# Second-vector modulation, pair seeding and gates moved between VectorE and ScalarE in a two-layer conv, attention and SwiGLU kernel

## The chip, the cores and the metric

The kernel runs on one core of a Trainium2 chip. The metric is the device time of one execution in microseconds (us), as the median of several runs. Engines are named as in the profile: PE (TensorE, matmuls), PEld (its weight loads), DVE (VectorE), ACT (ScalarE), POOL (GpSimd) and SP (SyncE, whose queue issues the large loads).

## The reference, cut to what matters

Two layers work on 256 latent tokens and 256 context tokens of width 1024. Each layer is a half-weighted SwiGLU, a mixer (a short convolution in layer 0, grouped attention in layer 1) and another half-weighted SwiGLU. Every block is modulated by nine vectors per layer that come from a condition vector: one for the latents (`c`) and one for the context (`c_ctx`).

```
mod  = (silu(c)     @ mod_w[i] + mod_b[i]).reshape(bsz, 3, 3, 1, D_MODEL)
modc = (silu(c_ctx) @ mod_w[i] + mod_b[i]).reshape(3, 3, D_MODEL)
h    = rms(t, g) * (1 + scale) + shift
y    = (silu(h @ w1) * (h @ w3)) @ w2          # hidden width 2816 = 22 blocks of 128
t    = t + 0.5 * gate * y                      # for the mixers: t + gate * y
```

In layer 1 the context is needed only as keys and values, so its last modulation vectors and its last SwiGLU are not computed. All of it is float32.

## The kernel before

The activations stay transposed on the chip: `x` is 128 partitions x 8 blocks of the width x 512 tokens, of which columns 0 to 255 are latents (s = 0) and 256 to 511 context (s = 1). A float32 product is made of three matmuls (`mm3`): every operand is split into a rounded high part on ACT and the rest on DVE (`split`), and high x high, high x low and low x high are summed in PSUM.

Weights are loaded by SP in pieces of 128 x 2048 (1 MB) into a raw buffer (`load_raw`, tag `wr`, three buffers) and split into halves of 1024 columns (`half`, four buffers).

An FFN goes through its 22 hidden blocks in thirds of 8, 7 and 7. After each third, `project` multiplies that third with the second weight matrix, eight output blocks m = 0 to 7 of 128 x 512 (tile `py`), and `finish` adds gate x result to `x`, one DVE operation for each vector's 256 columns. In the last third the blocks 6 and 7 are done in token halves (`late`), so that the next norm can begin; `square_add` and `rms_inv` make that norm's sums.

In three of the four FFNs most hidden blocks are a `Pair`: the gate and the up block of one hidden index are the two rows of a 2 x 2 block product over (gate, up) x (two halves of the width) and (latents, context), which is computed with seven block products and sums of blocks in place of eight. `sums` of `Pair` makes the weight sums (in a tile `ws` of their own), `sums` of `Blocks` those of the activations. A product is 12 matmuls of 256 columns. One pair uses two PSUM banks: p and q. `head` puts the first product (A11) into p, which ACT copies to SBUF, and the second (A12) into the first half of q; `five` puts S1 into the second half of q, which ACT copies to `gm`; `six` adds S2 onto p (copied by ACT) and S4 onto the second half of q, then DVE adds q and the copies over 512 columns and ACT takes the SiLU; `seven` adds S3 onto p, which DVE turns into the second half of the up block; `four` adds A22, and DVE multiplies. A pair's `seven` and `four` stand between the products of the next pair. The first hidden blocks of an FFN are plain products (`w13_mm`, `w13_post`).

The modulation vectors are made beside this on DVE. Transposed modulation weights come in 64 pieces of two 1024-wide parts (`modT`); a unit (`mod_unit`) multiplies a part with one broadcast vector and sums it in one operation (junk tile, accumulator `mod`), so a piece has four units, or two where only the latents need it: 224 in all. `tick(n)` grants n units at places in the program; `mod_ready` forces what is missing when a vector is asked for (`gate_of`, `scale_of`). Ticks stand after each `finish` (1.5 to 1.7 each), in the convolution (6 for each of 8 blocks), in the q/k/v part (1, 1, 2), with each of the eight heads (2) and in the attention's output projection (1 each).

The start is different: the first modulation vectors come from PE (`mod_pe`, `mod_turn`, loads `mod0`), mixed with the first three hidden blocks in an order written out by hand (`FIRST_STEPS`). Elsewhere a planner lays out each engine's instructions from the program's order and its own costs; it may put an instruction that is ready before one that is not. Each engine then runs its list in that order. PSUM has eight banks: six results (`psum`, tag `mm`) and two small ones (`psmall`).

Of the kernel before, what the change touches and what calls it, by code (L numbers as in the profile page):

```python
# [16 lines left out]
P = 128  # L17
# [24 lines left out]
def hybrid_kernel(ctx: ExitStack, tc: tile.TileContext, a: dict, out: bass.AP):  # L42
# [7 lines left out]
    psm = ctx.enter_context(tc.tile_pool(name="psm", bufs=6, space=bass.MemoryType.PSUM))  # L50
# [9 lines left out]
    def psum(s="ps"):  # L60
        return psm.tile([P, T2], F32, tag="mm", name=nm(s))
# [30 lines left out]
    def load_raw(src, n=2048):  # L92
        raw = wp.tile([P, 2048], F32, name=nm("wr"), tag="wr", bufs=3)
        nc.sync.dma_start(raw[:, :n], src)
        return raw
# [11 lines left out]
    def load_w(src, n=2048, fine=False):  # L107
        raw = load_raw(src, n)
        hs = [half() for _ in range(0, n, 1024)]
        cuts = (0, 1024, 512, 1536) if fine else range(0, n, 1024)  # L110
# [52 lines left out]

    jobs = [(0, ch, p) for ch in range(2, 9) for p in range(4)]
# [4 lines left out]
    def next_unit():  # L169
        if not units:  # L170
            l, ch, pair = jobs.pop(0)
            mod_tile(l, ch)
            raw = load_raw(a["modT"][l, ch * 4 + pair])
            units.extend(
                (l, ch, pair, raw, j, v) for j in range(2) for v in range(streams(l, ch))
            )
        mod_unit(*units.pop(0))

    def tick(n):

        owed[0] += n
        while (jobs or units) and owed[0] >= 1:
            owed[0] -= 1
            next_unit()
# [31 lines left out]
    def square_add(k, c0, c1):  # L216
# [4 lines left out]
        for s in range(2):  # L221
            if c0 <= s * S < c1:
                part = sq[:, s * S - c0 : s * S - c0 + S]
                if k == 0:
                    accs[s] = tp.tile([P, S], F32, name=nm("acc"), tag=f"acc{s}", bufs=1)
                    nc.vector.tensor_copy(accs[s], part)
                elif k < KT - 1:
                    nc.vector.tensor_tensor(out=accs[s], in0=accs[s], in1=part, op=ALU.add)
                else:
                    accs[s, "last"] = part  # L230
# [165 lines left out]
    def tail_norm(l, j, h):  # L396
# [3 lines left out]
        def tail(m, c0, c1):  # L400
            square_add(m, c0, c1)
            if m == KT - 1:
# [5 lines left out]
                def inv():  # L408
                    return rms_inv(s, (accs[s], accs[s, "last"]))
# [31 lines left out]
    def finish(m, ps, c0, c1, gate, tail):  # L441
        g = gate()
        for s in range(2):
            if c0 <= s * S < c1:
                o = s * S - c0
# [72 lines left out]

    def w13_mm(pp, w, h, ks, c0, c1):
        for k in ks:  # L520
            mv = pick(h, k, c0, c1)
            for i in range(2):
                mm3(pp[i][:, c0:c1], w((1 - i) * 1024 + k * P), mv, k == 0, k == KT - 1)
# [9 lines left out]
    class Pair:  # L533
# [6 lines left out]
        def __init__(self, src, h):  # L540
            self.h, self.w = h, {}
            self.raw = load_raw(src)
            self.keep(("A11", "A12"), self.raw[:, 1024:])
# [7 lines left out]
        def sums(self, n):  # L551

            a21, a22, a11, a12 = (self.raw[:, i * T2 : i * T2 + T2] for i in range(4))
            tt = nc.vector.tensor_tensor
            if n == 0:
                self.sm = sm = wp.tile([P, 2048], F32, name=nm("ws"), tag="ws", bufs=1)
                tt(
                    out=sm.rearrange("p (a b c) -> p a b c", a=2, b=2)[:, :, 0, :],
                    in0=a21.unsqueeze(1).to_broadcast([P, 2, T2]),
                    in1=self.raw[:, T2 : 3 * T2].rearrange("p (a c) -> p a c", a=2),  # L560
                    op=ALU.subtract,
                )
                tt(out=sm[:, T2:1024], in0=a11, in1=sm[:, :T2], op=ALU.subtract)
                self.keep(("S1", "S2"), sm[:, :1024])
                return
            sm = self.sm
            tt(out=sm[:, 3 * T2 :], in0=a12, in1=sm[:, T2:1024], op=ALU.subtract)
            self.keep(("S3", "S4"), sm[:, 1024:])
            self.w["A22"] = [
                wp.tile([P, T2], F32R, name=nm(t), tag=t, bufs=2) for t in ("w4h", "w4l")  # L570
            ]
            split(*self.w["A22"], a22)
# [6 lines left out]
        def head(self):  # L579
            p, q = psum("p"), psum("q")  # L580
            self.p, self.q, self.q1 = p[:, :S], q, q[:, S:]
# [612 lines left out]
```

## Time and profile before

| | us |
|---|---|
| median of 3 runs | 1596.06 (1595.92 to 1598.62) |
| span of the profiled execution | 1599.4 |
| PE busy | 1572.9 |
| DVE busy | 1304.2 |
| ACT busy | 718.6 |
| POOL busy | 29.7 |

The profiled execution's time is its span, from the first to the last instruction; the page shows nothing around it, and it lies 3.3 us above the median of the runs. Busy time is the union of an engine's instructions. A matmul's end is modelled: a matmul of 256 columns is shown for 0.28 us, though the next one starts 0.12 us after it, so short waits of PE are partly hidden in its busy time. In the groups, "idle before" is the engine's idle time just ahead of that group and what ended it. The granted clock is PE's, as a share of full speed.

### The profile page before, as it was taken

The numbers are of one execution on the slowest core, as the hardware profiler recorded it, in microseconds if no ns is written. First come the engines' busy times: TensorE is split into PE (matmuls) and PEld (weight loads), VectorE is DVE, ScalarE is ACT, GpSimd is POOL, SyncE is SP. The second block draws the span as 40 slices with busy tenths as digits, with TensorE's granted clock in tenths as the row PEclk, the third lists the DMA queues.
The fourth block names the chain that finished last, engine by engine and source line by source line (L and its number), as shares of the span: only waits on it lengthen the run. The fifth ranks groups of instructions, "written<-read, shape, count | busy, mean of one in ns | idle before, by whom it ended". The sixth has DMA issues, their size and how long they took to land.

```text
span 1599.4 us, 25805 instructions
## 1 busy us (share of the span) xinstructions
PE 1572.9 (98%) x10674; PEld 1452.2 (91%) x10674; DVE 1304.2 (82%) x1984; ACT 718.6 (45%) x1103; POOL 29.7 (2%) x20
## 2 busy tenths in 40 slices
PE   8999999999999999999999999999999998899999
PEld 6788998998888899999899899889899897899999
DVE  4778788879998879799798899898797799965554
ACT  5632452544322366335245375245254455554443
POOL 0000000000000000000000000000000005100000
PEclk9999999999999999999999999999999999989999
DMA  8455234234565422453443423452432554755462
GB/s 312 173 185 187 103 106 175 103 117 160 184 220 198 162 80 83 155 185 100 139 145 106 174 78 108 175 191 96 155 132 97 181 199 150 261 189 187 167 201 104
DMA packets 38422, 248.79 MB, mean 156 GB/s; under 512 B 5280, under 2 KB 7072, under 8 KB 12448
## 3 DMA queue, kind: packets, MB, share of 16 engines
q1 hardware_dynamic: 35712, 245.38, 44.0%
q10 hardware_dynamic: 2592, 1.76, 0.4%
q8 instruction: 83, 1.36, 0.3%
q14 instruction: 35, 0.29, 0.1%
HBM read 244.77 MB, written 1.05 MB: 154 GB/s over the span
## 4 chain that ended last, share of the span: by engine, by line
PE 87%; DVE 7%; DMA 3%; ACT 1%; issue 1%; POOL 0%; DVEq 0%; ACTq 0%; SPq 0%; POOLq 0%
PE py L122 8%; PE py L123 8%; PE py L124 8%; PE p L123 6%; PE p L122 6%; PE p L124 6%; PE q L124 5%; PE q L122 5%; PE q L123 5%; PE pg L122 3%; PE pg L123 3%; PE pg L124 3%; PE pu L124 3%; PE pu L123 3%; PE pu L122 3%; DVE junk L142 2%
## 5 line engine op out<-in xcount | busy, mean ns | idle before, releaser
L98 ACT ACTIVATE wh<-wr 128x1024 fp32r<-128x1024 f32 (+2 forms) x276 | 276.4, 1014 | 401.1 <-PE py L123 111.3
L99 DVE TENSOR_TENSOR wl<-wr,wh 128x1024 fp32r<-128x1024 f32 (+2 forms) x276 | 320.0, 1167 | 96.5 <-ACT wh L98 95.9
L142 DVE CUSTOM_DVE_ANT_0 junk<-wr,scbc,modb 128x1024 bf16<-128x1024 f32 x224 | 287.0, 1281 | 38.9 <-DMA wr<-in_modT 36.3
L122 PE MATMUL py<-gh,wh 128*128 128x512 f32 (+1 forms) x746 | 263.2, 353 | 0.0
L123 PE MATMUL py<-gl,wh 128*128 128x512 f32 (+1 forms) x746 | 263.1, 353 | 0.0
L124 PE MATMUL py<-gh,wl 128*128 128x512 f32 (+1 forms) x746 | 262.8, 352 | 0.0
L124 PEld LDWEIGHTS py<-gh,wl 128*128 128x128 f32 x746 | 141.1, 189 | 19.1
L122 PEld LDWEIGHTS py<-gh,wh 128*128 128x128 f32 x746 | 141.2, 189 | 18.5
L123 PEld LDWEIGHTS py<-gl,wh 128*128 128x128 f32 x746 | 141.2, 189 | 18.1
L99 DVE TENSOR_TENSOR wl<-ws,wh 128x1024 fp32r<-128x1024 f32 x108 | 131.8, 1224 | 29.1 <-ACT wh L98 28.9
L98 ACT ACTIVATE wh<-ws 128x1024 fp32r<-128x1024 f32 x108 | 113.5, 1058 | 68.0 <-PE p L123 35.5
L124 PE MATMUL p<-th,wl 128*128 128x256 f32 x432 | 122.2, 283 | 0.0
L123 PE MATMUL p<-tl,wh 128*128 128x256 f32 x432 | 122.2, 283 | 0.0
L122 PE MATMUL p<-th,wh 128*128 128x256 f32 x432 | 122.2, 283 | 0.0
L446 DVE SCALAR_TENSOR_TENSOR x<-py,G,x 128x256 f32<-128x256 f32 x168 | 74.1, 479 | 21.9 <-PE py L124 21.4
L122 PE MATMUL q<-bh,wh 128*128 128x256 f32 x320 | 90.6, 283 | 0.0
L123 PE MATMUL q<-bl,wh 128*128 128x256 f32 x320 | 90.6, 283 | 0.0
L124 PE MATMUL q<-bh,wl 128*128 128x256 f32 x320 | 90.6, 283 | 0.0
L122 PEld LDWEIGHTS p<-th,wh 128*128 128x128 f32 x432 | 82.9, 192 | 0.3
L123 PEld LDWEIGHTS p<-tl,wh 128*128 128x128 f32 x432 | 82.9, 192 | 0.3
L124 PEld LDWEIGHTS p<-th,wl 128*128 128x128 f32 x432 | 82.9, 192 | 0.0
L122 PE MATMUL pg<-hh,wh 128*128 128x256 f32 (+1 forms) x240 | 77.2, 322 | 3.7 <-ACT hh L266 3.6
(238 smaller groups left out, 4049.7 us busy)
## 6 DMA issues: line engine op xcount, KB each, us to landing
wr<-in_w SPq DMA_DIRECT2D x88, 1024.0 KB, 4.9
wr<-in_modT SPq DMA_DIRECT2D x64, 1024.0 KB, 4.9
wr<-in_w2b SPq DMA_DIRECT2D x32, 896.0 KB, 4.6
wr<-in_w2a SPq DMA_DIRECT2D x16, 1024.0 KB, 4.9
wr<-in_mod SPq DMA_DIRECT2D x8, 1024.0 KB, 6.7
wr<-in_cw_cx SPq DMA_DIRECT2D x8, 1024.0 KB, 5.0
wr<-in_cw_b SPq DMA_DIRECT2D x4, 1024.0 KB, 4.9
wr<-in_cw_out SPq DMA_DIRECT2D x4, 1024.0 KB, 4.9
```

The costliest lines, as they stand in the source:

```text
L98: nc.scalar.activation(out=hi, in_=src, func=AF.Copy)
L99: nc.vector.tensor_tensor(out=lo, in0=src, in1=hi.bitcast(F32), op=ALU.subtract)
L122: nc.tensor.matmul(ps, wh, mh, start=first, stop=False, **kw)
L123: nc.tensor.matmul(ps, wh, ml, start=False, stop=False, **kw)
L124: nc.tensor.matmul(ps, wl, mh, start=False, stop=last, **kw)
L142: nc.vector.tensor_tensor_reduce(out=junk, in0=raw[:, j * D : j * D + D], in1=scbc[:, v, :], scale=1.0, scalar=modb[:, l, col : col + 1], ...
L446: nc.vector.scalar_tensor_tensor(out=x[:, m, s * S : s * S + S], in0=ps[:, o : o + S], scalar=g[:, m, s : s + 1], in1=x[:, m, s * S : s * ...
```

## The change

- **Modulation.** Where a piece serves two vectors, the first keeps its two DVE units. The second is done by `mod_both`: DVE multiplies the whole piece in place with the second vector, 2048 columns in one operation, and ACT sums each part (Identity with an accumulator); the biases are added at the end of a chunk. `mod_both` counts as two units.
- **Ticks.** After a full-width result 2 (1.5 in an FFN's last third), 4.5 in place of 6 in the convolution, 1 in place of 2 in the third q/k/v place and with each head; half a tick with each pair, whose DVE work is placed behind the DVE add of `seven`.
- **Pair.** The first product goes into the first half of q; ACT copies it from there into p, onto which S2 is summed later. The second product is added onto the first half of q itself, and ACT takes that half's SiLU straight from PSUM; the DVE add covers only the other half. The order is now first product, previous pair's `seven`, second product and S1, previous pair's `four`, S2 and S4.
- **PSUM.** Six banks become two sides, a and b, of three; p is on side a, q on side b, other results take the sides in turn. In `w13_mm` only the first token half starts a fresh sum in the bank.
- **Gates.** `finish` on full-width results: ACT scales each half out of PSUM into a tile, and one DVE operation adds it to `x`. Halves are done as before.
- **Block sums** are made in the raw tile itself, and `ws` is gone; `wr` has four buffers. The up blocks of `w13` are stored with their halves exchanged, so that the parts lie where the sums want them. The norm's sums of squares are one tile for both vectors.

```
-    psm = ctx.enter_context(tc.tile_pool(name="psm", bufs=6, space=bass.MemoryType.PSUM))
+    psm = ctx.enter_context(tc.tile_pool(name="psm", bufs=3, space=bass.MemoryType.PSUM))
...
-    def psum(s="ps"):
-        return psm.tile([P, T2], F32, tag="mm", name=nm(s))
+    def psum(s="ps", side=None):
+        if side is None:
+            turns[0] += 1
+            side = "ab"[turns[0] % 2]
+        return psm.tile([P, T2], F32, tag=side, name=nm(s))
...
-        raw = wp.tile([P, 2048], F32, name=nm("wr"), tag="wr", bufs=3)
+        raw = wp.tile([P, 2048], F32, name=nm("wr"), tag="wr", bufs=4)
...
+    def mod_both(l, ch, pair, raw):
+        mt = mod_tile(l, ch)
+        r3 = raw.rearrange("p (j d) -> p j d", j=2)
+        nc.vector.tensor_tensor(
+            out=r3, in0=r3, in1=scbc[:, 1, :].unsqueeze(1).to_broadcast([P, 2, D]), op=ALU.mult
+        )
+        for j in range(2):
+            kt = pair * 2 + j
+            part = raw[:, j * D : j * D + D]
+            nc.scalar.activation(
+                out=part, in_=part, func=AF.Identity, accum_out=mt[:, kt, 1:2]
+            )
+        done[l, ch] += 2
+        if done[l, ch] == 16:
+            nc.vector.tensor_tensor(
+                out=mt[:, :, 1], in0=mt[:, :, 1], in1=modb[:, l, ch * KT : ch * KT + KT],
+                op=ALU.add,
+            )
...
-    def tick(n):
+    def tick(n, behind=None):
         owed[0] += n
         while (jobs or units) and owed[0] >= 1:
-            owed[0] -= 1
-            next_unit()
+            if behind is None:
+                owed[0] -= next_unit()
+            else:
+                with tc.issue_after(behind.ins):
+                    owed[0] -= next_unit()
...
     def finish(m, ps, c0, c1, gate, tail):
         g = gate()
+        if c1 - c0 == T2:
+            t = tp.tile([P, T2], F32, name=nm("fy"), tag="gm", bufs=3)
+            for s in range(2):
+                c = slice(s * S, s * S + S)
+                nc.scalar.activation(
+                    out=t[:, c], in_=ps[:, c], func=AF.Identity, scale=g[:, m, s : s + 1]
+                )
+            nc.vector.tensor_tensor(out=x[:, m, :], in0=x[:, m, :], in1=t, op=ALU.add)
...
         def sums(self, n):
...
+                tt(
+                    out=r4[:, 0::3, :], in0=a21.unsqueeze(1).to_broadcast([P, 2, T2]),
+                    in1=r4[:, 0::2, :], op=ALU.subtract,
+                )
+                tt(out=a22, in0=a22, in1=a11, op=ALU.subtract)
+                self.keep(("S2", "S1"), self.raw[:, 1024:])
...
-        def head(self):
-            p, q = psum("p"), psum("q")
-            self.p, self.q, self.q1 = p[:, :S], q, q[:, S:]
+        def one(self):
+            p, q = psum("p", "a"), psum("q", "b")
+            self.p, self.q0, self.q1 = p[:, :S], q[:, :S], q[:, S:]
             self.u = p
             self.sg = tp.tile([P, T2], F32, name=nm("sg"), tag="sg", bufs=3)
-            self.prod(self.p, "A11", ("B", 0, 0))
-            nc.scalar.copy(self.sg[:, :S], self.p)
-            self.prod(q[:, :S], "A12", ("B", 1, 0))
-
-        def five(self):
+            self.prod(self.q0, "A11", ("B", 0, 0))
+            nc.scalar.copy(self.p, self.q0)
+
+        def two_five(self):
+            self.prod(self.q0, "A12", ("B", 1, 0), False)
+            nc.scalar.activation(out=self.sg[:, :S], in_=self.q0, func=AF.Silu)
             self.prod(self.q1, "S1", "T1")
             self.gm = tp.tile([P, T2], F32, name=nm("gm"), tag="gm", bufs=3)
             nc.scalar.copy(self.gm[:, S:], self.q1)

         def six(self):
             self.prod(self.p, "S2", "T2", False)
-            nc.scalar.copy(self.sg[:, S:], self.p)
+            g = self.sg[:, S:]
+            nc.scalar.copy(g, self.p)
             self.prod(self.q1, "S4", ("B", 1, 1), False)
-            nc.vector.tensor_tensor(out=self.sg, in0=self.q, in1=self.sg, op=ALU.add)
-            nc.scalar.activation(out=self.sg, in_=self.sg, func=AF.Silu)
+            nc.vector.tensor_tensor(out=g, in0=self.q1, in1=g, op=ALU.add)
+            nc.scalar.activation(out=g, in_=g, func=AF.Silu)
...
-                        pr.head()
-                    pr.five()
+                        pr.one()
                     if prev:
-                        prev.seven()
-                    pr.six()
+                        tick(0.5, prev.seven())
+                    pr.two_five()
                     if prev:
                         gs.append(new_pair("g"))
                         prev.four(gs[-1])
+                    pr.six()
                     prev = pr
```

100 lines of the change are left out of this document (52 added, 48 removed).

## The prediction

> **What bounds the kernel now.** I read the page's busy shares and chain of waits first, then a table of stretches, then the waits inside the stretches that were left.
>
> ```profile
> span 1599.4 us, 25805 instructions
> PE 1572.9 (98%) x10674; PEld 1452.2 (91%) x10674; DVE 1304.2 (82%) x1984; ACT 718.6 (45%) x1103; POOL 29.7 (2%) x20
> PE 87%; DVE 7%; DMA 3%; ACT 1%; issue 1%; POOL 0%; DVEq 0%; ACTq 0%; SPq 0%; POOLq 0%
> ```
>
> TensorE is busy for 98% of the span and makes 87% of the chain. The change keeps every product (seven per block pair, three matmuls per weight block), so it can only win back time in which PE waits. That is 1599.4 - 1572.9 = 26.5 us, plus what a low clock costs around the waits. The stretches say where it lies (PE, PEld, DVE, ACT and POOL busy, granted clock, DMA share):
>
> ```profile
> 0.00:60.00 60.00, 53.36 (x363) 40.06 (x363) 27.90 (x71) 30.77 (x62) 0.19 (x4) 0.94 0.79 288
> 60.00:1000.00 940.00, 937.76 (x6071) 860.02 (x6071) 815.68 (x1190) 418.70 (x623) 0.00 (x0) 1.00 0.41 141
> 1000.00:1062.00 62.00, 60.24 (x327) 52.08 (x326) 56.00 (x86) 16.08 (x22) 0.00 (x0) 1.00 0.51 183
> 1062.00:1270.00 208.00, 207.83 (x1470) 196.04 (x1468) 176.44 (x252) 97.40 (x145) 0.00 (x0) 1.00 0.39 137
> 1270.00:1325.00 55.00, 54.38 (x402) 51.28 (x403) 47.45 (x86) 28.93 (x51) 0.00 (x0) 1.00 0.56 193
> 1325.00:1405.00 80.00, 68.20 (x475) 61.80 (x475) 75.20 (x160) 45.22 (x91) 29.52 (x16) 0.94 0.59 209
> 1405.00:1600.00 195.00, 191.12 (x1577) 190.92 (x1576) 105.49 (x143) 81.47 (x113) 0.00 (x0) 0.99 0.49 164
> ```
>
> Three stretches hold nearly all of it: the start (6.6 us idle), the head of the third FFN's first output projection (1.8), and attention with its output projection (11.8). In 60:1000 and 1062:1270, 1148 us together, PE idles 2.4 us. There the relief of VectorE is worth nothing, however large: the cover is PE's own stream. New waits of PE can arise there.
>
> **DVE and ACT, part by part.** Prices come from these groups (busy us, mean ns of one | idle before):
>
> ```profile
> L142 DVE CUSTOM_DVE_ANT_0 junk<-wr,scbc,modb 128x1024 bf16<-128x1024 f32 x224 | 287.0, 1281 | 38.9 <-DMA wr<-in_modT 36.3
> L142 DVE DVE_READ_ACCUMULATOR2_ANT mod<- 128x1 f32 x224 | 18.7, 83 | 0.0
> L99 DVE TENSOR_TENSOR wl<-wr,wh 128x1024 fp32r<-128x1024 f32 x200 | 243.3, 1221 | 70.2 <-ACT wh L98 69.6
> L446 DVE SCALAR_TENSOR_TENSOR x<-py,G,x 128x256 f32<-128x256 f32 x168 | 74.1, 479 | 21.9 <-PE py L124 21.4
> L597 DVE TENSOR_TENSOR sg<-q,sg 128x512 f32<-128x512 f32 x54 | 37.0, 685 | 0.3 <-PE q L124 0.2
> L602 DVE TENSOR_TENSOR p<-p,gm 128x256 f32<-128x256 f32 x54 | 23.3, 431 | 19.0 <-PE p L124 18.7
> L585 ACT COPY sg<-p 128x256 f32<-128x256 f32 x54 | 19.7, 365 | 16.8 <-PE p L124 16.8
> L98 ACT ACTIVATE wh<-ws 128x1024 fp32r<-128x1024 f32 x108 | 113.5, 1058 | 68.0 <-PE p L123 35.5 <-DVE ws L563 21.3 <-PE py L123 7.5
> ```
>
> Modulation: 48 of the 64 loaded pieces have two vectors. Two units of 1.281 + 0.083 = 2.73 us become one product of 2048 columns, which from 0.685 at 512 and 1.221 at 1024 I put at 2.29 us: DVE saves 0.44 x 48 = 21 us, ACT gains two summing passes of some 1.06 us each, 102 us. Gates: 66 full-width results in three FFNs and 6 in the convolution lose two operations of 0.479 for one of 0.685: 0.27 x 72 = 20 us off DVE, and 2 x 0.365 x 72 = 53 us on ACT. Block pairs: the add before the SiLU shrinks from 0.685 to 0.431, 0.25 x 54 = 14 us off DVE. Block sums done in place have the same shapes as now, so nothing. DVE falls to about 1249 us (78%), ACT rises to about 874 us (55%). Both stay under PE, so by themselves these sums move the end by 0.
>
> The ticks move more. Counting them in the code, attention and its output projection now take 28 units (junk); afterwards 15, all of the one-vector kind, the rest being done earlier, half a tick in each block pair, queued on VectorE behind that pair's add. A pair lasts 84 matmuls x 0.12 us (starts 640.38 and 640.50 below) = 10.1 us, and half a tick costs some 0.63 us of DVE (a two-vector piece counts four and costs 2 x 1.364 + 2.29 = 5.0), less the 0.25 saved. DVE is 85% busy in 1062:1270; this makes it 89%, still under PE. The pieces' loads move with the ticks, among the weight loads on SP; one piece then holds a raw buffer over some four pairs, which leaves the weights three of four, as many as they have now: 0.
>
> **The start.** A fourth raw buffer lets SP run one load further ahead.
>
> ```profile
> 9.70 7.38 SPq L94 DMA_DIRECT2D wr<-in_w  x3
> 22.18 0.69 DVE L99 TENSOR_TENSOR wl<-wr,wh 128x512 fp32r<-128x512 f32 x1
> 22.89 0.33 SPq L94 DMA_DIRECT2D wr<-in_mod  x1
> 14.83 1.86 PE pr L754 x32
> 22.89 7.78 DMA wr<-in_mod
> 30.81 1.94 PE pr L754 x16
> 34.34 0.23 PE pu L123
> 36.18 1.00 PE pr L754 x16
> L754 PE MATMUL pr<-wr,sccol 128*32 128x256 f32 x32 | 3.0, 509 | 2.5 <-DMA wr<-in_mod 2.5
> ```
>
> The load that PE waits for (2.5 us, until 30.81) is issued at 22.89, when the first weight's last split (22.18 + 0.69) frees a buffer three loads back. With four buffers it needs only the buffer that PE has read by 14.83 + 1.86 = 16.7. Issued there, behind one other load, it has over 11 us to PE's 28.3 and took 7.8. So the 2.5 us go. PE was also slow after the idling: its next 16 small matmuls took 1.94 us where the 16 at 36.18 take 1.00, and the 12 of 512 columns between 32.75 and 36.18 took 3.4 us against 12 x 0.23 (the row at 34.34). That is another 1.6 us. Next late is the norm chain that follows, which stays. I take 4 us; bounds 0 (DMA already at 0.79 of its engines) and 6.
>
> **Head of the third FFN's first projection.**
>
> ```profile
> L142 DVE CUSTOM_DVE_ANT_0 junk<-wr,scbc,modb 128x1024 bf16<-128x1024 f32 x22 | 28.2, 1280 | 1.1 <-DMA wr<-in_modT 0.8
> L124 PE MATMUL q<-th,wl 128*128 128x256 f32 x7 | 2.1, 296 | 1.3 <-DVE wl L99 1.3
> ```
>
> In 1000:1062 the gate forces 11 units at once and 22 pass through a DVE that is busy 56.0 of 62 us, so PE waits for a weight split. By the new ticks the gate is nearly complete when asked for. I take the 1.8 us of idle as gained; bounds 0 and 2.5.
>
> **Attention.** The groups of 1325:1405:
>
> ```profile
> L142 DVE CUSTOM_DVE_ANT_0 junk<-wr,scbc,modb 128x1024 bf16<-128x1024 f32 x21 | 26.8, 1277 | 1.0 <-DMA wr<-in_modT 1.0
> L1067 PE MATMUL pt<-ident,pn 128*128 128x128 f32 x64 | 9.7, 283 | 4.5 <-POOL pn L1058 3.0 <-DVE ptl L99 1.4
> L124 PE MATMUL py<-a,wl 128*128 128x256 f32 x64 | 17.8, 288 | 1.0 <-DVE wl L99 1.0
> L248 PE MATMUL ss<-ident,ri 128*128 128x128 f32 x4 | 1.2, 460 | 1.5 <-DVE ri L246 1.5
> ```
>
> DVE is busy 75.2 of 80 us here, 26.8 of them modulation. Nine fewer units take off 9 x 1.36 = 12 us. PE's waits for the transposes, the weight splits and the norm's reciprocal then shrink. The chain maximum, exponential, GpSimd's scaling, transpose stays, and so does the norm chain of the projection. Of 11.8 us idle I take 6.5, and 1.5 of the 4.8 us that a clock of 0.94 costs in 80 us: 8 us, bounds 2 and 14.
>
> **The new waits.** PE's order changes to first product, previous pair's S3, second product, S1, previous pair's A22, S2, S4.
>
> ```profile
> 640.38 0.28 PE L124 MATMUL q<-th,wl 128*128 128x256 f32 x1
> 640.50 0.28 PE L122 MATMUL p<-th,wh 128*128 128x256 f32 x1
> 640.70 0.38 ACT L591 COPY gm<-q 128x256 f32<-128x256 f32 x1 [0.50 <-PE q L124]
> 1053.04 0.28 PE L122 MATMUL q<-bh,wh 128*128 128x256 f32 x1
> 1053.66 0.39 PE L124 MATMUL p<-bh,wl 128*128 128x256 f32 x1 [0.22 <-DVE wl L99]
> ```
>
> A PE group that needs ScalarE to have read the last result would start 640.70 + 0.38 + 0.04 - 640.50 = 0.62 us late (0.04 is the step from PE's end at 640.66 to ScalarE's start) if nothing stood between. The second product accumulates on the half of q that ScalarE copies out, and the 12 matmuls of S3 (1.44 us) stand between: covered, unless ScalarE is in a 1.06 us split or behind one. The first pair of the second and third thirds has no S3 to cover it: 6 x 0.62 = 3.7 us, bounds 0 and 7.4 (if its SiLU wait is bare too). Queued behind that wait on PE is the whole pair.
>
> S1 writes the other half of q while ScalarE's SiLU reads the first half. No row of before shows PE writing one half of a bank while ScalarE reads the other, so the price lies between 0 and 0.62 for each of 54 pairs, 0 to 33 us. I take 0.05 each, 2.7 us, near the lower end, because of 1053.04 and 1053.66: where PE's next group was not ready, the order of issue had already put another group's matmuls in front (q before the rest of p), so the A22 group can fill this gap. The Trainium skill (PSUM — Partial Sum Buffer, section "PSUM bank collisions raise a hardware error") says that two engines must not touch one bank at the same time, whatever the columns; by that rule S1 has to wait for the SiLU in every pair, and without filler the sum would be up to 33 us worse.
>
> PSUM is now two sides of three banks instead of six; with results drawn in turn each side cycles as before, and gates read a bank through ScalarE (2 x 0.365) instead of VectorE (2 x 0.479), so banks come free no later: 0.
>
> **Sum.** -4 - 1.8 - 8 + 3.7 + 2.7 = -7.4 us against the profiled 1599.4, which lies 3.3 above the median of the runs, 1596.06 (1595.92 to 1598.62); the page gives nothing around the span. From the median: 1588.7, say 1589.
>
> **Rivals.** (1) Slower: the bank. S1 waits for the SiLU in each pair and the filler isn't there, because A22 waits for VectorE's add (0.431 us, queued behind splits of 1.22). Price 54 x 0.62 = 33 us at worst: 1596 - 13.8 + 3.7 + 33 = 1619; it decides from (13.8 - 3.7) / 54 = 0.19 us per pair. For it: PE's cover is exactly one group, and VectorE is 85% busy. Against it: reordering seen in the rows, and 1.4 us of A22 for a 0.6 us gap. A half-filled gap gives about 1603. (2) The gains fall short: the start is limited by bandwidth (0.79 of the DMA engines) and attention by GpSimd (29.5 us for 16 scalings). Then -1 - 1.8 - 3 + 3 = about 1593, no change to slightly faster. (3) The new waits are fully filled and attention loses all its DVE waits: -6 - 2 - 12 = 1576. (4) The edit doesn't do what its name says: seeding saves no matmul, and freeing VectorE frees no time of PE outside the three stretches. That is true already in my sum and gives nothing by itself; were the ticks' move the only thing that counts, -8 - 1.8 = 1586.
>
> **How the numbers follow.** Forecast, with (4), 0.52; (3) 0.13; (2) 0.15, half of it within 0.2%; (1) 0.20. About 0.2% (3.2 us) is what a measurement of this kernel can tell from no change. So faster 0.72, same 0.08, slower 0.20. The range goes from 1577 (nearly all of (3)) to 1605 (the half-filled gap of (1)); the forecast's own is 1582 to 1593.
>
> **What would show it.** Right: no wait for a modulation load near 28 us; 1325:1405 with DVE under 65 us and PE idle about 5; no forced modulation near 1025; PE idle in 60:1000 up by some 5 us, at first pairs of thirds. Wrong: PE idle of 0.2 us or more before the S1 group (q<-th) in each pair, with ScalarE as releaser; a start where PE still waits for a load; attention as long as now with GpSimd as releaser.

## The result, and the profile after

The changed kernel takes 1614.4 us (median of four runs, 1612.14 to 1616.97) where the kernel before takes 1597.3: a ratio of 1.010, 95% interval 1.0082 to 1.0117, some 16 us slower. The profiled execution took 1614.06 us. I had forecast 1589.0 and a range of 1577 to 1605.

The page of the changed kernel, span and busy shares:

```profile
span 1612.3 us, 26055 instructions
PE 1583.8 (98%) x10674; PEld 1454.1 (90%) x10674; DVE 1269.0 (79%) x1749; ACT 884.6 (55%) x1493; POOL 26.1 (2%) x20
```

VectorE fell to 79% and ScalarE rose to 55%, near the forecast (78%, 55%), though VectorE lost only 35 us where 55 were forecast (1304.2 to 1269.0 against 1249). TensorE is "busy" 10.9 us longer than before with the same 10674 matmuls, and idle only 28.5 us instead of 26.5. So nearly all of the 12.9 us that the span grew stands in the busy column. The span of the kernel before is itself a long one: in every run that lists both, an execution's time is 1.7 to 2.1 us above its span (1614.06 against 1612.3 here), so the profiled execution of before took some 1601 us by this estimate, 4 to 5 us above its medians and not 3.3. The stretches of the changed kernel (PE, PEld, DVE, ACT, POOL busy, granted clock, DMA share, GB/s) show no large idle time either, except in attention:

```profile
0.00:60.00 60.00, 54.40 (x373) 41.19 (x374) 29.81 (x71) 32.35 (x66) 0.19 (x4) 0.94 0.85 315
60.00:590.00 530.00, 527.15 (x3061) 467.39 (x3060) 428.33 (x559) 286.04 (x482) 0.00 (x0) 0.99 0.43 150
590.00:940.00 350.00, 346.32 (x2403) 322.44 (x2403) 301.37 (x383) 211.44 (x362) 0.00 (x0) 1.00 0.39 136
1338.00:1418.00 80.00, 70.30 (x523) 64.73 (x522) 64.54 (x135) 48.62 (x95) 25.89 (x16) 1.00 0.44 145
```

The groups of 60 to 1325 us say where to look. First the kernel before, then the changed one (busy us, mean ns of one | idle before):

```profile
L122 PE MATMUL q<-bh,wh 128*128 128x256 f32 x320 | 90.6, 283 | 0.0
L122 PE MATMUL q<-th,wh 128*128 128x256 f32 x216 | 61.3, 284 | 0.2 <-ACT wh L98 0.2
```
```profile
L128 PE MATMUL q<-bh,wh 128*128 128x256 f32 x480 | 136.4, 284 | 1.6 <-ACT p L629 1.1 <-ACT wh L104 0.5
L128 PE MATMUL q<-th,wh 128*128 128x256 f32 x216 | 66.7, 309 | 2.0 <-ACT wh L104 1.4 <-ACT sg L633 0.3
```

One group became dearer: q<-th,wh, the matmuls of S1, 284 to 309 ns at the same count. One pair of the changed kernel on PE, its weight loads and ScalarE, in three answers (start, duration):

```profile
181.78 0.28 PE L130 MATMUL q<-hh,wl 128*128 128x256 f32 x1
181.90 0.28 PE L128 MATMUL p<-th,w4h 128*128 128x256 f32 x1
182.10 0.38 ACT L633 ACTIVATE sg<-q 128x256 f32<-128x256 f32 x1 [0.45 <-PE q L130]
182.26 0.28 PE L128 MATMUL p<-th,w4h 128*128 128x256 f32 x1
182.54 0.39 PE L128 MATMUL q<-th,wh 128*128 128x256 f32 x1
182.76 0.28 PE L129 MATMUL q<-tl,wh 128*128 128x256 f32 x1
```
```profile
182.14 0.19 PEld L128 LDWEIGHTS p<-th,w4h 128*128 128x128 f32 x1
182.54 0.19 PEld L128 LDWEIGHTS q<-th,wh 128*128 128x128 f32 x1 [0.20 <-ACT sg L633]
```

The second product's last matmul starts at 181.78. The SiLU on that half of q runs from 182.10 to 182.48, and S1, which writes the other half, starts at 182.54. Only four of the twelve matmuls of the A22 group (181.90 to 182.26) stand in the gap of 0.76 us; they follow the second product at the usual pace, and the other eight come behind S1. So S1 starts 0.28 us after the matmul before it where the pace is 0.12 (0.16 lost), and the next one follows after 0.22 (0.10 lost): 0.26 us. In 42 of the 54 pairs four matmuls stand there, and in 38 of these S1 is 0.16 late. A matmul lasts 0.28 us at a pace of 0.12, so the gap is covered by the overlap: PE's rows show no idle time, only the weight load's do. This is the bank rule that the prediction quoted from the Trainium skill (PSUM — Partial Sum Buffer, section "PSUM bank collisions raise a hardware error"); the trace agrees in that S1 does wait for a reader of other columns of its bank, and it gives the price, 0.26 us a time. The wait is one that the program makes by a semaphore, and no run leaves it out, so what the chip would do without it is not shown.

As the idle columns hide this, I counted lateness from the trace instead: each matmul's start less the start of the one before, less the pace (0.120 us at 256 columns, 0.227 at 512, 0.112 below), where over 0.02 us is left. In us, by stretch (bounds in each kernel's own time):

```
stretch               before  after | e2 pairs  e9 S1 first | e5 sums  e10 w4x3 | e13   e15 | e6 ticks
0-100     start        18.4   16.3      14.3       15.3        16.3      18.0     16.9  16.3    15.6
150-350   pairs         0.1    4.8       5.7        0.9         2.7       0.2      2.7   6.9     0.0
350-450   seam          1.9    6.3       1.1        1.1         1.1       1.9      3.5   3.4     0.7
550-650   head          3.8    6.1       4.8        3.6         7.3       7.2      3.9   5.1     2.5
650-900   pairs         0.0    4.8       5.6        0.9         2.7       0.0      2.2   6.1     0.0
900-1000  head          2.6    5.5       6.5        7.0         8.7       9.6      7.0   6.3     4.6
1000-1250 pairs         2.5    5.4       6.5        1.9         3.1       7.8      2.2   7.2     0.0
1250-1450 attention    24.7   18.1      21.2       23.5        22.7      22.1     23.0  20.1    22.3
sum                    54.1   67.3      65.7       54.4        64.5      66.8     61.4  71.4    45.8
```

The sum grows by 13.2 us, which is nearly the span's 12.9. It holds waits and also time at a low granted clock. Each column is one execution, and some are not typical of their kernel: that of before is some 4 us long, that of e10 is 4.9 us above its median, that of e2 3.5 us below. Pairs, heads of FFNs and the convolution's seam lose; start and attention win.

### The profile page after: what moved, and what is told of

The parts are those of the page before. It is cut to its first block, busy times and chain, and to the rows that moved or that the text cites. A ratio compares the mean times of both kernels' runs of the same rounds, so it can differ in the third digit from the quotient of the medians.

```text
span 1612.3 us, 26055 instructions
## 1 busy us (share of the span) xinstructions
PE 1583.8 (98%) x10674; PEld 1454.1 (90%) x10674; DVE 1269.0 (79%) x1749; ACT 884.6 (55%) x1493; POOL 26.1 (2%) x20
## 5 line engine op out<-in xcount | busy, mean ns | idle before, releaser
L105 DVE TENSOR_TENSOR wl<-wr,wh 128x1024 fp32r<-128x1024 f32 (+2 forms) x384 | 448.7, 1183 | 164.5 <-ACT wh L104 163.1
L104 ACT ACTIVATE wh<-wr 128x1024 fp32r<-128x1024 f32 (+2 forms) x384 | 391.6, 1028 | 291.1 <-PE py L129 85.6
L148 DVE CUSTOM_DVE_ANT_0 junk<-wr,scbc,modb 128x1024 bf16<-128x1024 f32 x128 | 163.9, 1281 | 19.7 <-DMA wr<-in_modT 18.6
L128 PE MATMUL q<-bh,wh 128*128 128x256 f32 x480 | 136.4, 284 | 1.6 <-ACT p L629 1.1
L129 PE MATMUL q<-bl,wh 128*128 128x256 f32 x480 | 135.7, 283 | 0.0
L180 ACT ACTIVATE wr<-wr 128x1024 f32<-128x1024 f32 x96 | 101.0, 1055 | 61.2 <-DVE wr L174 40.1
L174 DVE TENSOR_TENSOR wr<-wr,scbc 128x2048 f32<-128x2048 f32 x48 | 109.8, 2287 | 0.7
L128 PEld LDWEIGHTS q<-bh,wh 128*128 128x128 f32 x480 | 92.1, 192 | 3.0 <-ACT p L629 2.1
L129 PEld LDWEIGHTS q<-bl,wh 128*128 128x128 f32 x480 | 92.1, 192 | 0.2
L130 PEld LDWEIGHTS q<-bh,wl 128*128 128x128 f32 x480 | 91.8, 192 | 0.0
```

What stands on the lines that cost most here:

```text
L104: nc.scalar.activation(out=hi, in_=src, func=AF.Copy)
L105: nc.vector.tensor_tensor(out=lo, in0=src, in1=hi.bitcast(F32), op=ALU.subtract)
L128: nc.tensor.matmul(ps, wh, mh, start=first, stop=False, **kw)
L129: nc.tensor.matmul(ps, wh, ml, start=False, stop=False, **kw)
L130: nc.tensor.matmul(ps, wl, mh, start=False, stop=last, **kw)
L148: nc.vector.tensor_tensor_reduce(out=junk, in0=raw[:, j * D : j * D + D], in1=scbc[:, v, :], scale=1.0, scalar=modb[:, l, col : col + 1], ...
```

## The experiments

Times are medians beside runs of the kernel before on the same chip; ratios are to that kernel, and 0.1% is 1.6 us. Runs e1 to e8, e9 to e12 and e13 to e15 were on three chips, so across these groups only ratios are compared. The theory after the result was: the S1 wait on the bank is the main loss. The rival was: ScalarE, with 166 us more to do, is late everywhere, and S1 is only where it shows.

**S1 ahead of the SiLU, in the changed kernel (e1).**

```diff
             self.prod(self.q0, "A12", ("B", 1, 0), False)
-            nc.scalar.activation(out=self.sg[:, :S], in_=self.q0, func=AF.Silu)
             self.prod(self.q1, "S1", "T1")
+            nc.scalar.activation(out=self.sg[:, :S], in_=self.q0, func=AF.Silu)
```

> Changed kernel, with the product S1 issued ahead of ScalarE's SiLU instead of behind it, so that S1 (which writes the other half of the same PSUM bank) no longer waits for the SiLU; the SiLU then waits for S1. Nothing else moves. Theory 1 (the bank): the trace of the changed kernel shows 5.9 us at the first S1 matmul and 5.7 us at its second, 11.6 us over 54 pairs; they go, and the time falls from 1614.4 to about 1603 (1600 to 1606). Theory 2 (ScalarE is late everywhere, by its 166 us of added work): the wait only moves to the next product that needs a ScalarE read, S4 behind the copy of S1; the time stays within 4 us of 1614, with 8 us or more of PE idle ahead of q<-bh,wh.

1606.9 us, 1.0052 (1.0034 to 1.0070): 7.5 us back, less than the 11.5 that both S1 gaps sum to. The waits at S1 in the pairs went, and 3.7 us came in at four later pairs (0.78 to 1.22 us each), where the second product waits for ScalarE's copy of the first behind two weight splits. One of them, on ScalarE in e1:

```profile
768.46 2.00 ACT L104 ACTIVATE wh<-wr 128x1024 fp32r<-128x1024 f32 x2 [0.18 <-DVE wr L612]
770.37 0.36 ACT L629 COPY p<-q 128x256 f32<-128x256 f32 x1
```

So theory 1 held in kind and theory 2 in a part (a wait did move to another product that needs a ScalarE read), and 9 us of loss were left.

**The new pair order alone, in the kernel before (e2), and the same with S1 ahead (e9).** The edit is the functions one, two_five, six and seven and the two sides of PSUM; e9 moves the SiLU as in e1 and takes over the start rule of w13_mm. Without that rule e2 loses the copied first product in some pairs; its instructions are the same.

> Kernel before, with only the new order of a block pair's products (first product into q and copied to p by ScalarE, SiLU straight from q, S1 behind it, two sides of three banks); modulation, gates, block sums, buffers and ticks as before. Theory 1 (the bank): 12 us of waits at S1 and 3.2 us at the first pairs come with the order, whatever else ScalarE does: 1597.3 + 15 = 1612 (1608 to 1615). Theory 2 (ScalarE is late): with ScalarE at 45% instead of 55% its SiLU is on time and the gap is filled by the previous pair's last product: only the first pairs' 3.2 us and a little, 1600 to 1604.

> Kernel before, with the new order of a block pair's products, but S1 ahead of the SiLU (and the products' start rule of the changed kernel, which the copied first product needs). Against the run with the new order alone (1615.7) only the order of S1 and SiLU differs. Theory 1 (the bank is the price of the new order): the 11 us of waits at S1 go, the first pairs of the thirds still wait some 4 us for the copy of their first product: 1597.5 + 5 = 1602 (1600 to 1605). Theory 2 (the new order costs by something else, such as the two sides of three banks): 1610 or more.

e2: 1615.7 us, 1.0111 (1.0091 to 1.0132). e9: 1601.5 us, 1.0020 (1.0008 to 1.0032). The order alone costs 17.7 us, as much as the whole change, with ScalarE at 45% of the span: its added work is not needed for it. And 14.5 of those us, by the two ratios, hang on one line, SiLU ahead of S1 or behind (the start rule apart). The groups of e2, then of e9, 60 to 1325 us:

```profile
L128 PE MATMUL q<-th,wh 128*128 128x256 f32 x216 | 66.1, 306 | 2.3 <-ACT sg L595 0.8
```
```profile
L128 PE MATMUL q<-bh,wh 128*128 128x256 f32 x480 | 136.6, 285 | 4.2 <-ACT p L591 4.2
L128 PE MATMUL q<-th,wh 128*128 128x256 f32 x216 | 61.2, 283 | 0.0
```

S1 is back at 283 ns with no wait, and what e9 still loses is the 4.2 us for the copy at first pairs. So S1's wait for the SiLU, with which it shares only the bank, is shown as the main price of the new order.

How many matmuls stand in the gap does not set that price. In 33 of e2's 54 pairs ScalarE begins the SiLU only 0.93 to 0.94 us after the second product's end, behind a weight split, and eleven matmuls stand ahead of S1 where the changed kernel has four. S1 is still 0.19 us late (ScalarE, then PE, in e2):

```profile
190.79 1.06 ACT L104 ACTIVATE wh<-ws 128x1024 fp32r<-128x1024 f32 x1 [0.43 <-PE q L129]
191.75 0.36 ACT L595 ACTIVATE sg<-q 128x256 f32<-128x256 f32 x1
```
```profile
191.86 0.28 PE L129 MATMUL p<-tl,w4h 128*128 128x256 f32 x1
192.17 0.38 PE L128 MATMUL q<-th,wh 128*128 128x256 f32 x1
```

In both kernels S1 starts 0.05 us behind the SiLU's end, and its place in PE's list comes 0.16 to 0.19 us too early, whether eight A22 matmuls are left behind it or one. In the changed kernel two more of them ahead of S1 (0.24 us) would have covered the wait by this estimate; no run tried it, and why the list puts S1 there is not shown.

**The old pair order, with all the rest of the change (e3).** The edit puts head, five, six and seven back.

> Changed kernel, with the order of a block pair's products put back to the one before (first product into p and copied out, one add and one SiLU over 512 columns), and all the rest of the change kept: ScalarE sums, gates, sums in place, four buffers, ticks. Theory 1 (the bank): 12 + 3.2 us go: 1614.4 - 15 = 1599 (1596 to 1602). Theory 2 (ScalarE is late): what is left still has ScalarE's added work, and so most of the loss: 1608 or more.

1604.9 us, 1.0037 (1.0025 to 1.0050). 10 us come back, not 15. S1 is late here too (0.12 us in 34 pairs, 0.10 at its second matmul), though nothing reads its bank: it starts 0.05 us behind ScalarE's split of its own weights. So a second cause was there, which led to e5.

**Block sums in place and the fourth buffer alone, in the kernel before (e5), then with three buffers for A22's weights (e10).**

```diff
-                self.sm = sm = wp.tile([P, 2048], F32, name=nm("ws"), tag="ws", bufs=1)
+                split(*self.w["A22"], a22)
...
-                tt(out=sm[:, T2:1024], in0=a11, in1=sm[:, :T2], op=ALU.subtract)
+                tt(out=a22, in0=a22, in1=a11, op=ALU.subtract)
...
-            split(*self.w["A22"], a22)
```
```diff
-                    wp.tile([P, T2], F32R, name=nm(t), tag=t, bufs=2) for t in ("w4h", "w4l")
+                    wp.tile([P, T2], F32R, name=nm(t), tag=t, bufs=3) for t in ("w4h", "w4l")
...
-        raw = wp.tile([P, 2048], F32, name=nm("wr"), tag="wr", bufs=4)
+        raw = wp.tile([P, 2048], F32, name=nm("wr"), tag="wr", bufs=3)
```

> Kernel before, with only the block sums done in place over their blocks (A22 split first, since its block is overwritten) and the fourth raw buffer that the freed space pays for. In the changed kernel with the old pair order, S1 started 0.12 us late in 34 pairs and its second matmul 0.1 us late, right behind ScalarE's split of the S2 and S1 weights. Theory 1 (the chain of sums in place makes that split late by itself): the same wait is here, 8 us, and 4 us at the heads of the thirds, less at most 2 to 4 us at the start: 1597.6 + 9 = about 1606 (1602 to 1609). Theory 2 (it is late because ScalarE also sums and gates): no such wait here: 1594 to 1598.

> Block sums in place as in the run that had them alone (1610.8), with three buffers for A22's split weights instead of two, paid for by going back to three raw buffers. Theory 1 (A22's split has to come first because the sum overwrites its block, and it waits for the A22 product of the pair before last to free its buffer, so that the S1 weights come late): the wait at S1 in the pairs goes (10 us), 3 to 5 us stay at the heads of the thirds, where the chain itself is longer: 1600 to 1604. Theory 2 (the sums are late because they wait for the split of A11 and A12, whose block they overwrite too): 1608 or more.

e5: 1610.8 us, 1.0078 (1.0060 to 1.0096). e10: 1608.8 us, 1.0070 (1.0054 to 1.0086). A pair of e5 (PE, ScalarE, VectorE and again PE):

```profile
1082.08 0.28 PE L124 MATMUL p<-th,w4l 128*128 128x256 f32 x1
```
```profile
1082.30 0.62 ACT L98 ACTIVATE w4h<-wr 128x512 fp32r<-128x512 f32 x1
1084.45 2.27 ACT L98 ACTIVATE wh<-wr 128x1024 fp32r<-128x1024 f32 x2 [0.24 <-DVE wr L569]
```
```profile
1083.01 0.69 DVE L99 TENSOR_TENSOR w4l<-wr,w4h 128x512 fp32r<-128x512 f32 x1
1083.73 0.69 DVE L569 TENSOR_TENSOR wr<-wr 128x512 f32<-128x512 f32 x1
```
```profile
1085.32 0.28 PE L124 MATMUL p<-th,wl 128*128 128x256 f32 x1
1085.57 0.39 PE L122 MATMUL q<-th,wh 128*128 128x256 f32 x1
1085.79 0.28 PE L123 MATMUL q<-tl,wh 128*128 128x256 f32 x1
```

A22's block is overwritten by a sum, so A22 has to be split first; its split buffer comes free only when the A22 product of the pair before last is through (last matmul 1082.08); then split, subtraction, sum and the split of the S2 and S1 weights follow one another up to 1085.5, and S1 starts late at 1085.57. With three A22 buffers the lateness within the pairs goes (table: 150-350 from 2.7 to 0.2, 650-900 from 2.7 to 0.0), as theory 1 said. The time does not follow and lies in theory 2's range: by the ratios e10 is only 1.3 us under e5. Its trace shows 2.7 us lost in one wait for a weight split at 1067 and 1.7 more than e5 at the start, but that execution was the slowest of six, 4.9 us above the median, and e10 has one raw buffer fewer besides. So the mechanism in the pairs is shown; its worth in time by itself is not.

**Single other parts, in the kernel before: units (e6), gates (e7), ScalarE sums (e8); and ScalarE sums taken out of the changed kernel (e4).**

For e6, e7 and e8 the edits are the change's own lines for tick and ev, for finish, and for mod_both with its weights. For e4:

```diff
-                units.append((2, lambda: mod_both(l, ch, pair, raw)))
+                for j in range(2):
+                    units.append((1, lambda j=j: mod_unit(l, ch, pair, raw, j, 1)))
```

> Kernel before, with only the new places of the modulation units: half a unit in each block pair behind the pair's add, fewer in attention (units as before, one weight each). Theory 1 (the units in attention cost 6 us there, and a half unit in a pair nothing): 1597.6 - 6 - 1.5 = 1590 (1588 to 1592), with PE idle 2 us or less in the pairs. Theory 2 (with three buffers the modulation piece that is held over eight pairs leaves the weights two): the pairs wait for weight loads or splits, 1600 or more.

> Kernel before, with only the full-width gates done by ScalarE (two scaled copies out of PSUM) and one add of 512 columns on VectorE. Theory 1 (off the path): within 2 us of 1597.6. Theory 2 (a scaled copy sits behind 1.06 us splits on ScalarE, so banks come free later and the split for the next weights slips): 1601 or more, with PE waits ahead of py groups.

> Kernel before, with only the second vector's modulation done as one product of 2048 columns on VectorE and two summing passes on ScalarE (units weighted 1, 1 and 2; ticks at their old places). Undoing it in the changed kernel gave 3 us back, 4.4 us of it at the convolution's seam. Theory 1 (the sums cost only where a norm waits behind them): 1597.6 + 3 to 5 = 1601 to 1603, lost at the seams at 360 to 410, 930 to 970 and 1300. Theory 2 (VectorE's relief pays for it): within 2 us of 1597.6 or below, attention 4 us shorter.

> Changed kernel, with the second vector's modulation back on VectorE (two units of 1.28 us each instead of one 2.29 us product and two ScalarE sums of 1.06 us), everything else as changed. ScalarE loses 102 us of work, VectorE gains 20. Theory 1 (the bank): the pairs' waits stay nearly whole, since the SiLU has to come first by whatever order; only the sums in the seams go (4.5 us at the convolution): 1608 to 1612. Theory 2 (ScalarE is late): the waits at S1 fall by half or more and the seams too: 1600 to 1605.

e6: 1593.8 us, 0.9973 (0.9962 to 0.9984). e7: 1598.7, 1.0002 (0.9991 to 1.0013). e8: 1600.9, 1.0023 (1.0011 to 1.0035). e4: 1611.2, 1.0079 (1.0061 to 1.0097). Moving the units wins 4.3 us, half of what I had booked for it; gates cost nothing; ScalarE sums cost 3.7 alone, and taking them out of the changed kernel gives back about as much. Their loss there is at the convolution's seam. ScalarE, then PE, in the changed kernel:

```profile
393.81 1.06 ACT L104 ACTIVATE wh<-wr 128x1024 fp32r<-128x1024 f32 x1
394.77 1.04 ACT L180 ACTIVATE wr<-wr 128x1024 f32<-128x1024 f32 x1
395.72 0.19 ACT L180 ACTIVATION_READ_ACCUMULATOR wr<-wr 128x1 f32 x1
395.81 0.49 ACT L301 ACTIVATE hh<-t,mod 128x256 fp32r<-128x256 f32 x1
```
```profile
396.36 0.39 PE L128 MATMUL pv<-hh,wh 128*128 128x256 f32 x1 [1.79 <-ACT hh L301]
```

A summing pass takes 1.04 us, and its read 0.19 more, ahead of the norm's result hh that PE waits for. In e4 hh follows the split directly, and PE's wait there is 0.19 us. In e8 the summing passes cost little at that seam (lateness 2.2 us against 1.9 before); more is lost at 550 to 650 (1.6 us over before), 900 to 1000 (0.8) and 1000 to 1250 (1.0). So the seams of 930 to 970 and 1300 that theory 1 named are shown for a part of the 3.7 us at most.

**More units in the pairs (e11), and units with gates (e12).** 0.8 for 0.5 in each pair; e6 and e7 together.

> Kernel before with the new places of the modulation units alone (1593.8), with 0.8 units in each block pair instead of 0.5, so that no unit is left for attention. Theory 1 (attention still loses time to the units there): PE idle of 22 us from 1250 to 1405 falls by 3 to 6 us: 1588 to 1591. Theory 2 (what is left in attention is its own chain of maximum, exponential, scaling and transpose, and the pairs' VectorE is full): 1593 to 1597.

> Kernel before with the new places of the modulation units and the gates by ScalarE, the two parts of the change that cost nothing by themselves (1593.8 and 1598.7). Theory 1 (the parts add up, the gates at nothing): 1594 to 1595. Theory 2 (the relief of VectorE by the gates, 20 us, shortens the output projections' norms where units no longer stand in the way): 1590 to 1592.

e11: 1596.3 us, 0.9984 (0.9973 to 0.9995): attention loses 3.6 us less (22.3 to 18.7 by start times), but in 1150 to 1200 the pairs wait 5.2 us, mostly for weight splits, and the time is in theory 2's range. e12: 1599.8 us, 1.0009 (0.9996 to 1.0021), both of my theories missed: two parts of -4.3 and +0.3 us gave +1.4 together. The lateness is spread (start, a first pair at 816, the heads, the norm behind attention), and why the gates undo the gain is left open.

**How the causes combine (e13, e14, e15).** The changed kernel with the sums out of place and three raw buffers: with S1 ahead (e13), with S1 ahead and VectorE's modulation (e14), with neither (e15).

> Changed kernel with S1 ahead of the SiLU (1606.9) and, besides, the block sums out of place again, with three raw buffers. Theory 1 (bank and sums in place are the two causes of the loss): the 10 us of PE idle at the heads (600 to 650 and 950 to 1000) go: 1606.9 - 8 = 1599 (1597 to 1601). Theory 2 (what is left at the heads comes from ScalarE's added work, not from the sums): 1604 or more, with the idle still at the heads.

> The same with the second vector's modulation back on VectorE as well; of the change there remain the new pair order with S1 ahead, the gates by ScalarE and the places of the units. Theory 1: another 3 us less (the seam at 360 to 410), 1595 to 1597, at or under the kernel before. Theory 2 (ScalarE's gates and copies alone keep the loss): 1600 or more.

> Changed kernel with only the block sums out of place again and three raw buffers; S1 still behind the SiLU. Theory 1 (two causes that overlap little in this order, since S1 comes 24 matmuls later than in the old order and so covers the late sums within the pairs): only the heads gain, 1614.4 - 7 = 1607 (1605 to 1610), and the waits of 0.26 us per pair stay. Theory 2 (the waits at S1 in the changed kernel come from the late sums, not from the bank): they go, 1600 or less.

e13: 1607.9 us, 1.0050 (1.0037 to 1.0063). e14: 1602.0, 1.0022 (1.0012 to 1.0031). e15: 1619.4, 1.0124 (1.0106 to 1.0143). The sums do make the heads late: with S1 ahead the lateness of 600 to 650 falls from 6.0 (e1) to 1.7 us, that of 950 to 1000 from 4.1 to 1.7. But the time stays, so theory 1 held for the stage and missed the sum: other waits come. e15 is 4 us slower than the changed kernel by the ratios, above the ranges of both its theories. One of the new waits, on ScalarE in e15:

```profile
282.16 2.00 ACT L104 ACTIVATE wh<-ws 128x1024 fp32r<-128x1024 f32 x2
284.05 0.38 ACT L628 COPY p<-q 128x256 f32<-128x256 f32 x1
```

The copy that PE's second product needs stands behind two weight splits, and PE loses 1.9 us at 284.48 where the changed kernel lost 0.4; in e13 this copy costs 5.1 us at three first pairs. Whether the splits' new order or the missing fourth buffer brings these waits is not shown, since both runs change the two together. The S1 lateness within pairs stays in e15 (table: 6.9, 6.1, 7.2), so there it comes from the bank and not from late sums. e14 gains 4.5 us over e13, as theory 1 said of this step, but ends 0.2% above the kernel before, in theory 2's range: new order with S1 ahead, gates and units cost +3.2 (e9), +0.3 and -4.3 us alone and +3.5 together, a shortfall of 4.3 us as against 5.4 in e12. But e14 also holds a part of the change that no run has alone, the norm's sums of squares in one tile for both vectors; what it does to the start is shown below.

The account: alone, the parts cost +17.7 (order), +12.5 (sums, with the fourth buffer), +3.7 (ScalarE sums), +0.3 (gates) and -4.3 us (units), +29.9 together; the change costs 16. About 9.2 of the difference are e5's S1 waits within pairs (38 of 0.13 us and 42 of 0.10), which the new order covers, since S1 comes after another group there. Another 3.8 are what the sums and the fourth buffer together win in the changed kernel (e15 against it); that this is the buffer's doing is not shown, as no run has the buffer without the sums. All of this is arithmetic over runs and not an experiment of its own, it leaves out the one-tile sums of squares, and e12 shows that parts need not add.

The fastest kernel of the study is e6, the kernel before with the units' new places alone: 1593.8 us, 0.27% under the kernel before and 1.3% under the changed one.

## Why the prediction was wrong

**The step that failed: "The new waits", 54 pairs x 0.05 = 2.7 us.** The mechanism was named, its bounds (0 to 0.62) held, and the point from which it decides (0.19 us a pair) was right: the pair loses 0.26 to 0.27 (14.5 us / 54 between e2 and e9; 0.16 + 0.10 in the rows). Wrong was where I set the value, 0.05. I had taken two rows in which PE's order had put other matmuls into a gap as evidence that the A22 group fills this one; the row shows four of twelve matmuls ahead of S1, 0.48 us of the 0.64 needed. That matmuls are at hand does not mean that the list puts enough of them in front: with eleven there S1 was late by as much (e2). And I priced only the gap, not the second matmul that follows late behind an exposed weight load. My own sign of "wrong", PE idle of 0.2 us ahead of S1, would have been missed by whoever looked at PE's idle times: it shows in the weight load's.

**A step left out: "Block sums done in place have the same shapes as now, so nothing."** Same shapes, another order of dependence. A22's split moved from the end of the chain to its head, behind a buffer that comes free late. Alone, with the fourth buffer, it costs 12.5 us, and no rival of mine had it. In the changed kernel its cost in time is not shown: taking it out again left the time as it was with S1 ahead (e13 against e1) and made it 4 us longer without (e15). What it does there is to make the heads late: S1's first matmul there waited 1.42 us for its weights' high part and 0.59 for the low part.

```profile
608.37 0.39 PE L128 MATMUL q<-th,wh 128*128 128x256 f32 x1 [1.42 <-ACT wh L104]
609.70 0.39 PE L130 MATMUL q<-th,wl 128*128 128x256 f32 x1 [0.59 <-DVE wl L105]
```

**Start, -4: about 0.** The wait of 2.5 us for a modulation load was that of one execution. Of the eight traces with three buffers and the same start, four have a wait near 28 us (2.5, 1.3, 1.1 and 1.1 us) and four have none. e2, without a wait, then e6 (PE, small products):

```profile
28.01 0.42 PE L762 MATMUL pr<-wr,sccol 128*32 128x256 f32 x4
```
```profile
29.20 1.07 PE L758 MATMUL pr<-wr,sccol 128*32 128x256 f32 x16 [1.33 <-DMA wr<-in_mod]
```

The second norm's first product starts at 36.2 in e2, 36.3 in e7, 37.4 in e6, all with three buffers, at 40.3 in the profiled execution of before, and at 38.1 in the changed kernel with four. The sign I named (no wait for a load near 28 us) is there, and what it wins is lost ahead of it, by a part of the change that I put at nothing: the norm's sums of squares in one tile (PE in the changed kernel):

```profile
12.14 0.38 PE L272 MATMUL ss<-ones,acc 128*128 128x1 f32 x2 [1.27 <-DVE acc L258]
15.79 2.97 PE L800 MATMUL pr<-wr,sccol 128*32 128x256 f32 x32
```

PE waits 0.9 to 1.4 us for this sum in all seven kernels that make it in one tile, and at most 0.1 us in the ten others. In those seven the granted clock is then at half for 3.4 us, and the 32 small matmuls, which take 1.9 us in before, take 2.9 to 3.5. No run has the one tile alone, so its worth over the whole kernel is open. That the profiled execution lay above the median was the hint, and I scaled the result by it instead of asking which stretch held the difference.

**Attention, -8, and the third FFN's head, -1.8: -4.3 together.** By start times attention's lateness falls by 6.6 us in the changed kernel and 2.4 in e6. VectorE came under 65 us in the stretch as said (64.54), but PE still idles 9.7 us there, not 5: of the 6.5 us of idle time that I took, 2.1 came. Most of the other 4.5 us is, by estimate, the clock: between 1250 and 1450 it was at half for 13.6 us in the execution of before and for 3.4 us in that of the changed kernel, and whether the change did that is not shown. The wait in the pairs near 1050 did go. My three stretches held 20.2 of the 26.5 us of idle time and not nearly all; 3.3 more lie behind 1405.

**First pairs of thirds, +3.7:** right in kind, 2.6 in size: the six pairs wait 0.41 to 0.47 us in the changed kernel where I had 0.62. That e9's groups show 4.2 and 0.4 us is not the same sum; most of it are two waits of 1.6 us at the first pairs of the first thirds, which I had not counted.

**DVE and ACT, "by themselves these sums move the end by 0":** right for the gates alone (+0.3), wrong for the summing passes (+3.7). I had compared totals of engines. At the convolution's seam in the changed kernel what counted was what stood ahead of the norm's result on an engine that works in order.

**Rival (1), the bank,** at a chance of 0.20, was what happened, but not for its reason: A22 did not wait for VectorE's add, its first four matmuls run at pace ahead of S1 (from 181.90). "A half-filled gap gives about 1603" had the loss nearly right, half of 0.62 against 0.27 measured; the 11 us above that are the start and attention gains that did not come, the heads and the seam.

## What to carry to other kernels

When TensorE is the bound, look at what each of its groups must wait for, not at the load of the engines that are relieved: in this program two halves of one PSUM bank are one resource to a writer and a reader, a product that could fill a gap is worth only what the order list puts there, and an operation done in place turns a free order into a chain. A wait that is shorter than the overlap of pipelined matmuls is not in the idle column; look at the mean duration of a group, at the weight loads' idle time and at start-to-start times. Before booking a DMA wait of one execution as a gain, ask whether other executions have it. And price every part of a change, the small ones too.

## What was not expected of the hardware

- A matmul that waits even briefly costs 0.10 us more than its wait: its weight load starts with it (both at 182.54) instead of ahead of it, it is shown for 0.39 instead of 0.28 us, and the next one starts 0.22 us later instead of 0.12. This held alike for waits of 0.16 us on ScalarE's SiLU (the changed kernel) and 0.13 us on a weight split (e5).
- The same load at the start landed early or late from run to run: PE waited 2.52, 1.33 and 0 us for it in the kernel before, e6 and e2, whose starts have the same instructions.
- After PE's wait of 0.9 to 1.4 us at 12 us the granted clock was at half for 3.4 us in all seven kernels that had this wait; the ten others had no half clock before 30 us, not even e5 after a wait of 1.1 us at 16.7. Why is open.
- A scaled copy of 256 columns out of PSUM took ScalarE 0.47 us (the changed kernel's gates), where a plain copy takes 0.365 and VectorE's multiply and add 0.479. I had used the plain copy's price.
